# Conditioning vectors as VectorE dot products along rows of a transposed weight, in a two-block transformer kernel

## The chip, the cores and the metric

One core of a Trainium2 chip runs the whole program in one launch. The metric is the device time of one execution in microseconds. The kernel before takes 3524.61 us (median of three runs, 3524.37 to 3529.66). Engines are called as the profile calls them: PE (TensorE matmul), PEld (its weight load), DVE (VectorE), ACT (ScalarE), POOL (GpSimd), SP (SyncE, which issues the transfers).

## What is computed

`first_block` runs two layers on an image stream x (512 tokens by 1024) and a context stream of 256 tokens; `second_block` follows and is not touched. What the change is about is the conditioning: in each layer the vectors `c` and `c_ctx` pass through silu and are multiplied by `ada_w[l]` (1024 by 6144). The result, plus a bias, is cut into six vectors of 1024 that shift, scale and gate the two streams.

```python
for l in range(DEPTH):
    mod = (jax.nn.silu(c) @ ada_w[l] + ada_b[l])[:, None, :]
    sh1, sc1, g1, sh2, sc2, g2 = jnp.split(mod, 6, axis=-1)
    modc = jax.nn.silu(c_ctx) @ ada_w[l] + ada_b[l]
    shc1, scc1, gc1, shc2, scc2, gc2 = jnp.split(modc, 6, axis=-1)
    h = modulate(rms_norm(x, mix_pre_g[l]), sh1, sc1)
    hc = modulate(rms_norm(xc, mix_pre_g[l]), shc1, scc1)
    ...
    x = x + g1 * rms_norm(y, mix_post_g[l])
    h2 = modulate(rms_norm(x, ffn_pre_g[l]), sh2, sc2)
    x = x + g2 * rms_norm(sq_relu_mlp(h2, w_ff1[l], w_ff2[l]), ffn_post_g[l])
```

In the last layer only x is carried on, and of the context's six vectors only the first two are needed.

## The kernel before

Every large product is done in fp32 by three fp32r matmuls (`mm3`, L236 to L238): each operand is split into a high and a low part. A weight tile of 128x1024 (512 KB) is loaded by SP into a buffer `wr` (there are four, shared by everything that is called `wr`), ACT casts it into `wh` (L212), DVE subtracts to get `wl` (L215), and PE then runs 24 matmuls with it. `wh` and `wl` have four buffers each. SP issues in program order, so a load that waits for a buffer holds up the loads behind it.

Layer 0 runs in this order: the conditioning for the first norm (the first four column groups), keys and values, the mixer on x (about 120 to 725 us), the mixer on the context (about 800 to 1100 us), and the feed-forward on both (to about 1560 us). During the mixer on x the split weights are also written to DRAM (`wmode` "store"); the mixer on the context reads them back, 1 MB for each weight, straight into `wh` and `wl` or, for one in three, into two `wr` buffers (`wmode` "load"), and DVE has no `wl` to make there. The mixer's depthwise convolution of 31 taps is DVE work (L767), one instruction for each tap of each 128 channels.

The conditioning is in `ada_jobs`. A column group is 512 of the 6144 columns; a job `chunk` loads a 512 KB `wr` tile and multiplies it on PE against the silu vectors (L429, `ada`), four chunks to a group; then DVE copies the sums (L434), PE transposes them (L440, `adat`), and DVE folds and biases them into `mod` (L446, L447). Layer 0's groups 4 to 11 are spread through the mixer on x, among the convolution's jobs; layer 1's twelve groups are spread through layer 0's feed-forward. Background jobs are queued by `spread` and released by `tick` as the foreground weights go by; a scheduler then sets the final order on each engine.

In the feed-forward (`ff`), an up step runs one weight on both streams, and the result goes through ACT (relu, square), POOL (square in fp32, L932) and DVE (the low part, L935); a down step adds into `fy` on DVE (L950). The temporaries `relu`, `sq` and `csg` share a pair of buffers with tag `e`.

The lines of the code are quoted by program below.

## Time and profile before

| | |
|---|---|
| median of three runs | 3524.61 us (3524.37 to 3529.66) |
| the profiled execution | 3527.21 us, span 3525.4 us, granted PE clock 0.985 |
| PE busy | 3419.6 us, 97% |
| DVE busy | 2046.7 us, 58% |
| ACT, POOL busy | 1418.6 us (40%), 845.6 us (24%) |
| `ada` loads | 96 of 512 KB, 4.7 us to landing (median) |

Busy time is the time in which an engine has an instruction running. Matmuls overlap, and their ends are modelled, so what a matmul costs is read from the distance between two starts. The chain of waits follows the work that ended last backward from the end of the program.

### The profile page before, as it was taken

What the parts mean: (1) busy time and instruction counts of PE and PEld (TensorE: products, weight loads), DVE (VectorE), ACT (ScalarE), POOL (GpSimd) and SP (SyncE); (2) the same over time, 40 slices, a digit from 0 to 9 for tenths busy, and PEclk for the clock granted to TensorE, in tenths of its full rate; (3) what the DMA queues carried; (4) which work ended last, traced back from release to release, by engine and by line L of the source; (5) the groups of instructions that cost most, each with busy time, mean ns of one, the idle gap of its engine ahead of it and who ended that gap; (6) DMA issues with size and microseconds to landing.
All of it is one profiled execution on the core that took longest, in us unless ns stands there. A gap on an engine that the chain in (4) does not pass through costs nothing.

```text
span 3525.4 us, 54772 instructions
## 1 busy us (share of the span) xinstructions
PE 3419.6 (97%) x21313; PEld 2997.6 (85%) x21313; DVE 2046.7 (58%) x3652; ACT 1418.6 (40%) x2472; POOL 845.6 (24%) x931
## 2 busy tenths in 40 slices
PE   6999999989999999999899999999999899999999
PEld 4897887889999888899888898898888877789888
DVE  5567779656574323346757879756333757674334
ACT  4562332444223331234565243345323545544223
POOL 3230021232113110114421021234002336442002
PEclk8999999999999999999999999999999999999999
DMA  8527879786995533343411222244333420054333
GB/s 287 185 73 259 311 273 333 287 321 253 349 355 214 169 118 119 122 143 131 151 37 37 96 96 87 93 147 134 98 100 110 139 95 1 1 168 121 99 98 120
DMA packets 176419, 557.90 MB, mean 158 GB/s; under 512 B 18464, under 2 KB 43424, under 8 KB 176032
## 3 DMA queue, kind: packets, MB, share of 16 engines
q1 hardware_dynamic: 176160, 554.41, 45.6%
q8 instruction: 168, 2.75, 0.3%
q14 instruction: 91, 0.75, 0.1%
HBM read 436.89 MB, written 117.44 MB: 157 GB/s over the span
## 4 chain that ended last, share of the span: by engine, by line
PE 91%; ACT 3%; DVE 2%; DMA 2%; POOL 1%; issue 1%; SPq 0%; POOLq 0%; ACTq 0%; DVEq 0%
PE f L236 12%; PE f L238 12%; PE f L237 12%; PE pg L236 3%; PE pb L236 3%; PE pg L237 3%; PE pg L238 3%; PE pb L238 3%; PE pb L237 3%; PE c L236 2%; PE c L238 2%; PE c L237 2%; PE ada L429 1%; PE wo L236 1%; PE wo L237 1%; PE wo L238 1%
## 5 line engine op out<-in xcount | busy, mean ns | idle before, releaser
L212 ACT CAST wh<-wr 128x1024 fp32r<-128x1024 f32 (+1 forms) x486 | 508.8, 1049 | 1240.4 <-PE f L237 500.7
L215 DVE TENSOR_TENSOR wl<-wr,wh 128x1024 fp32r<-128x1024 f32 (+1 forms) x486 | 629.3, 1296 | 538.5 <-ACT wh L212 530.3
L767 DVE SCALAR_TENSOR_TENSOR yx<-gl,pcol,yx 128x512 f32<-128x512 f32 x480 | 368.0, 770 | 10.3
L932 POOL TENSOR_TENSOR relu<-relu 128x512 f32<-128x512 f32 (+1 forms) x146 | 137.9, 946 | 904.3 <-ACT hxh L931 592.7
L236 PE MATMUL f<-hxh,wh 128*128 128x512 f32 x576 | 226.0, 394 | 0.0
L238 PE MATMUL f<-hxh,wl 128*128 128x512 f32 x576 | 223.7, 389 | 0.0
L237 PE MATMUL f<-hxl,wh 128*128 128x512 f32 x576 | 223.6, 389 | 0.0
L236 PE MATMUL f<-hx2h,wh 128*128 128x512 f32 (+1 forms) x584 | 213.4, 369 | 1.1 <-ACT hx2h L317 1.0
L238 PE MATMUL f<-hx2h,wl 128*128 128x512 f32 (+1 forms) x584 | 212.2, 365 | 0.0
L237 PE MATMUL f<-hx2l,wh 128*128 128x512 f32 (+1 forms) x584 | 211.9, 364 | 0.0
L950 DVE TENSOR_TENSOR fyx<-f,fyx 128x256 f32<-128x256 f32 x144 | 56.1, 420 | 173.1 <-PE f L238 173.0
L278 POOL TENSOR_TENSOR sm<-sm,mhalf 128x2 f32<-128x2 f32 (+4 forms) x89 | 91.9, 1035 | 252.5 <-DVE sm L276 248.0
L236 PEld LDWEIGHTS f<-hxh,wh 128*128 128x128 f32 x576 | 108.1, 188 | 28.1 <-issue 5.4
L236 PEld LDWEIGHTS f<-hx2h,wh 128*128 128x128 f32 x584 | 110.2, 190 | 23.2 <-issue 2.1
L238 PEld LDWEIGHTS f<-hxh,wl 128*128 128x128 f32 x576 | 108.1, 188 | 22.9
L237 PEld LDWEIGHTS f<-hxl,wh 128*128 128x128 f32 x576 | 108.2, 188 | 21.8
L238 PEld LDWEIGHTS f<-hx2h,wl 128*128 128x128 f32 x584 | 110.8, 190 | 17.5
L237 PEld LDWEIGHTS f<-hx2l,wh 128*128 128x128 f32 x584 | 110.7, 190 | 16.5
L592 POOL TENSOR_SCALAR p<-p,sm 128x768 f32<-128x768 f32 (+1 forms) x80 | 65.7, 821 | 204.9 <-DVE sm L591 162.3
L935 DVE TENSOR_TENSOR hxl<-relu,hxh 128x512 fp32r<-128x512 f32 (+1 forms) x90 | 55.3, 616 | 101.5 <-POOL relu L932 101.5
L679 POOL TENSOR_TENSOR mx<-mx,sg 128x512 f32<-128x512 f32 x32 | 50.9, 1591 | 263.8 <-DVE sg L678 263.8
L236 PE MATMUL f<-h4h,wh 128*128 128x512 f32 (+1 forms) x328 | 112.5, 343 | 0.0
(718 smaller groups left out, 10622.8 us busy)
## 6 DMA issues: line engine op xcount, KB each, us to landing
wr<-in_w_ff_dram SPq DMA_DIRECT2D x234, 512.0 KB, 3.5
wr<-in_w_in_dram SPq DMA_DIRECT2D x141, 512.0 KB, 3.9
wr<-in_ada_w_dram SPq DMA_DIRECT2D x96, 512.0 KB, 4.7
wd<-wh SPq DMA_DIRECT2D x96, 512.0 KB, 3.9
wd<-wl SPq DMA_DIRECT2D x96, 512.0 KB, 4.2
wr<-wd SPq DMA_DIRECT2D x64, 512.0 KB, 4.6
wh<-wd SPq DMA_DIRECT2D x64, 512.0 KB, 4.1
wl<-wd SPq DMA_DIRECT2D x64, 512.0 KB, 5.1
```

The costliest lines, as they stand in the source:

```text
L212: nc.scalar.copy(hi, raw)
L215: eng.tensor_tensor(lo, raw, hi.bitcast(F32), ALU.subtract)
L236: mm(ps, a[0], b[0], start=start, stop=False)
L237: mm(ps, a[0], b[1], start=False, stop=False)
L238: mm(ps, a[1], b[0], start=False, stop=stop)
L278: nc.gpsimd.tensor_tensor(r, v, self.mhalf[0:rows].to_broadcast([rows, n]), ALU.pow)
L592: nc.gpsimd.tensor_scalar(p[:, :W], p[:, :W], rc, 1.0, op0=ALU.mult, op1=ALU.mult)
L679: nc.gpsimd.tensor_tensor(merged.k(k), merged.k(k), sg.k(k), ALU.add)
L767: nc.vector.scalar_tensor_tensor(Y.k(k), src, w, Y.k(k), op0=ALU.mult, op1=ALU.add)
L932: nc.gpsimd.tensor_tensor(r, r, r, ALU.mult)
L935: nc.vector.tensor_tensor(lo.k(k)[:, o], r[:, a - c0:b - c0], hi.k(k)[:, o].bitcast(F32), ALU.subtract)
L950: nc.vector.tensor_add(y.k(k), p, y.k(k))
```

## The change

Only layer 0's first four column groups stay on PE. All other vectors are made by `ada_dot_jobs`: the weight is laid out transposed (`ada_wt`), so that a 128x1024 tile has 128 output columns on its partitions and all 1024 inputs along each row. A silu vector is broadcast to all partitions in two tiles `crow` of 512, which take the place of the rope tables `cos` and `sin` until those are loaded again. One job loads the next tile and makes two `tensor_tensor_reduce` on DVE with the tile loaded a job earlier, each over 512 elements with a running sum; the product itself goes to a `junk` tile with tag `e`. In the program each of the two is an instruction of 128x512 and one of 128x1 that reads the sum out (both stand as ISA).

There are 24 such jobs for x in the mixer on x, 24 for the context in the mixer on the context, and 80 in layer 0's feed-forward, where they start after the second pass instead of the first and are spread over 41 ticks instead of 45.

```diff
-    def ada_jobs(self, l, c0, c1):
+    def ada_jobs(self, c0, c1):
...
+    def ada_dot_jobs(self, *sets):
+        nc = self.nc
+        row, raws = [], []
+
+        def cond(x):
+            row[:] = [self.lp.tile([P, S], F32, tag=f"rope{u}", name=self.nm("crow")) for u in range(2)]
+            for u in range(2):
+                nc.sync.dma_start(row[u], self.I["crow"][x, u].partition_broadcast(P))
+                nc.scalar.activation(row[u], row[u], AF.Silu)
+
+        def load(l, x, c):
+            raw = self.wp.tile([P, KT * P], F32, tag="wr", bufs=NB["wr"], name=self.nm("wr"))
+            nc.sync.dma_start(raw, self.I["ada_wt"][l, c])
+            raws.append(raw)
+
+        def dot(l, x, c):
+            raw = raws.pop(0)
+            part = self.small(1)
+            acc = self.pcol[l][:, PC_ADAB + c:PC_ADAB + c + 1]
+            for u in range(2):
+                junk = self.e("junk")
+                dst = part if u == 0 else self.mod[l][:, c // 4, x, c % 4:c % 4 + 1]
+                nc.vector.tensor_tensor_reduce(junk, raw[:, u * S:(u + 1) * S], row[u], 1.0, acc,
+                                               ALU.mult, ALU.add, dst)
+                acc = part
+
+        todo = [(l, x, c) for l, x, c0, c1 in sets for c in range(c0, c1)]
+
+        def step(i):
+            if i < len(todo):
+                load(*todo[i])
+            if i and (i == 1 or todo[i - 1][1] != todo[i - 2][1]):
+                cond(todo[i - 1][1])
+            if i:
+                dot(*todo[i - 1])
+        return [lambda i=i: step(i) for i in range(len(todo) + 1)] + [row.clear]
...
-            if n == 0:
-                self.spread(jobs, 45.0)
+            if n == (0 if extra else 1):
+                self.spread(jobs, 45.0 if extra else 41.0)
...
-        jobs = self.ada_jobs(0, 0, 4)
+        jobs = self.ada_jobs(0, 4)
...
-            mg = self.mixer(sx, l, h[0], kvs, self.ada_jobs(0, 4, 12) if not last else (), folds)
+            mg = self.mixer(sx, l, h[0], kvs, self.ada_dot_jobs((0, 0, 16, 40)) if not last else (),
+                            lambda: folds(0))
...
-                mg = self.mixer(sc, l, h[1], [kvc], beside=list(pre))
+                mg = self.mixer(sc, l, h[1], [kvc], self.ada_dot_jobs((0, 1, 16, 40)), lambda: folds(1),
+                                beside=list(pre))
...
-                        self.ada_jobs(1, 0, 12) if not last else ())
+                        self.ada_dot_jobs((0, 1, 40, 48), (1, 1, 0, 16), (0, 0, 40, 48), (1, 0, 0, 48))
+                        + [self.setup_rope] if not last else ())
```

The folds of the vectors with the norms' gains move with them: those for x and for the context are made apart, and `G2` at the feed-forward's end.

On DVE, in the second up phase of layer 0's feed-forward, the order before is this (`hxl` and `hcl` are the low parts of the two streams' hidden values, `wl` the low part of the next weights, `adarow` the old conditioning):

```order
L935 TENSOR_TENSOR hxl_2557_13443<-relu_13438,hxh_2556_13440 128x512
L434 COPY adarow_13557<-ada_13317 128x256
L935 TENSOR_TENSOR hcl_2561_13475<-relu_13470,hch_2560_13472 128x256
L215 TENSOR_TENSOR wl_13645<-wr_13642,wh_13644 128x1024
L215 TENSOR_TENSOR wl_13722<-wr_13719,wh_13721 128x1024
L935 TENSOR_TENSOR hxl_2570_13525<-relu_13520,hxh_2569_13522 128x512
```

And this is the same place after the change (`junk` is the product of a dot, `sm` the sum of its first half, `mod` the finished column):

```order
L975 TENSOR_TENSOR hxl_2701_13227<-relu_13222,hxh_2700_13224 128x512
L215 TENSOR_TENSOR wl_13276<-wr_13273,wh_13275 128x1024
L483 ISA junk_13262,sm_13261<-wr_13184,crow_12576,pcol_93 128x512
L483 ISA sm_13261 128x1
L975 TENSOR_TENSOR hcl_2686_13175<-relu_13254,hch_2685_13172 128x256
L483 ISA junk_13264,mod_95<-wr_13184,crow_12577,sm_13261 128x512
L483 ISA mod_95 128x1
L483 ISA junk_13269,sm_13268<-wr_13259,crow_12576,pcol_93 128x512
L483 ISA sm_13268 128x1
L483 ISA junk_13271,mod_95<-wr_13259,crow_12577,sm_13268 128x512
L483 ISA mod_95 128x1
L215 TENSOR_TENSOR wl_13360<-wr_13357,wh_13359 128x1024
```

Between two `wl` there now stand three halves of dots or more. Moreover the program gives `wr_13357` the buffer of `wr_13259`, whose dot stands directly ahead of `wl_13360`, and gives `wr_13273` the buffer of `wr_13177`, whose dot stands directly ahead of the `hxl` above; this pattern repeats every two weights through the up phases.

On SP, in the mixer on the context, the loads before are only the stored weights, two for each weight:

```order
L205 DMA wh_9361<-wd_3946 128x1024
L205 DMA wl_9363<-wd_3947 128x1024
L205 DMA wh_9426<-wd_4177 128x1024
L205 DMA wl_9428<-wd_4178 128x1024
L205 DMA wr_9430<-wd_4187 128x1024
L205 DMA wr_9432<-wd_4188 128x1024
```

After the change a conditioning tile is queued among them:

```order
L205 DMA wh_9301<-wd_3911 128x1024
L205 DMA wl_9303<-wd_3912 128x1024
L473 DMA wr_9241<-in_ada_wt_dram 128x1024
L205 DMA wh_9373<-wd_4134 128x1024
L205 DMA wl_9375<-wd_4135 128x1024
L205 DMA wr_9297<-wd_3901 128x1024
```

Some six to nine stored tiles stand between two conditioning tiles there.

## Rows read from the trace of the kernel before

**Rows 1.** The page's first part: busy time, share of the span and instructions.

```profile
PE 3419.6 (97%) x21313; PEld 2997.6 (85%) x21313; DVE 2046.7 (58%) x3652; ACT 1418.6 (40%) x2472; POOL 845.6 (24%) x931
```

**Rows 2.** The page's fourth part: the chain that ended last, by engine.

```profile
PE 91%; ACT 3%; DVE 2%; DMA 2%; POOL 1%; issue 1%; SPq 0%; POOLq 0%; ACTq 0%; DVEq 0%
```

**Rows 3.** Windows of three stages: stretch, length, busy us by engine, PEclk, DMA, GB/s.

```profile
290.00:650.00 360.00, 360.00 (x1945) 292.81 (x1944) 287.54 (x418) 110.13 (x158) 40.26 (x45) 1.00 0.85 309
...
850.00:1090.00 240.00, 238.59 (x1991) 238.39 (x1992) 148.71 (x355) 56.95 (x130) 28.14 (x44) 1.00 0.94 346
...
1170.00:1520.00 350.00, 350.00 (x2178) 292.53 (x2178) 97.14 (x206) 83.78 (x133) 29.95 (x35) 1.00 0.39 126
```

**Rows 4.** Windows of the tile `ada` alone: PE, PEld, DVE; eight records to a chunk.

```profile
290.00:650.00 360.00, 18.93 (x232) 5.22 (x232) 3.34 (x8) 1.00 0.85 309
...
1090.00:1170.00 80.00, 5.50 (x60) 1.46 (x60) 0.42 (x1) 1.00 0.46 155
1170.00:1520.00 350.00, 25.35 (x324) 7.29 (x324) 4.67 (x11) 1.00 0.39 126
```

**Rows 5.** Timeline of PE around one chunk in the feed-forward: start, us, what.

```profile
1395.07 0.28 PE L237 MATMUL f<-hcl,wh 128*128 128x256 f32 x1
1395.19 0.28 PE L238 MATMUL f<-hch,wl 128*128 128x256 f32 x1
1395.40 0.64 PE L429 MATMUL ada<-wr,adast 128*32 128x256 f32 x8
1395.97 0.50 PE L236 MATMUL f<-hx2h,wh 128*128 128x512 f32 x1
1396.31 0.39 PE L237 MATMUL f<-hx2l,wh 128*128 128x512 f32 x1
1396.54 0.40 PE L238 MATMUL f<-hx2h,wl 128*128 128x512 f32 x1
```

**Rows 6.** Windows of the tile `adat` alone, mixer on x: PE, PEld, DVE.

```profile
290.00:650.00 360.00, 3.04 (x16) 2.17 (x16) 2.98 (x32) 1.00 0.85 309
```

**Rows 7.** DVE instructions near to a dot: by line (ns min/median/max), and timeline.

```profile
L767 DVE SCALAR_TENSOR_TENSOR yx<-gl,pcol,yx x480: 737/752/1782, 275.6 to 2236.8; 128x512 f32<-128x512 f32 x160
...
L591 DVE RECIPROCAL sm<-sm x80: 152/164/167, 125.8 to 1900.2; 128x1 f32<-128x1 f32 x80
...
511.99 3.10 DVE L767 SCALAR_TENSOR_TENSOR yx<-gl,pcol,yx 128x512 f32<-128x512 f32 x4
...
0.79 0.06 DVE L371 MEMSET mhalf<- 128x1 f32 x1 [0.79 <-PEq L2053]
```

**Rows 8.** DVE in the mixer on x by line: busy us, mean ns, idle before.

```profile
L215 DVE TENSOR_TENSOR wl<-wr,wh 128x1024 fp32r<-128x1024 f32 x59 | 77.4, 1312 | 39.6 <-ACT wh L212 37.1 <-PE sv L714 1.2 <-DMA wd<-wl 1.0
```

**Rows 9.** Two windows of 10 us, columns as in rows 3.

```profile
530.00:540.00 10.00, 10.00 (x56) 7.51 (x56) 10.00 (x14) 5.02 (x6) 2.60 (x2) 1.00 0.75 264
...
990.00:1000.00 10.00, 10.00 (x86) 10.00 (x85) 9.41 (x21) 0.39 (x1) 1.75 (x2) 1.00 0.99 369
```

**Rows 10.** Transfers from 850 to 1090 us.

```profile
DMA packets 23062, 83.16 MB, mean 346 GB/s; under 512 B 2560, under 2 KB 2560, under 8 KB 23040
```

**Rows 11.** Timeline of SP, ACT and DVE in the feed-forward around one weight.

```profile
1414.34 0.33 SPq L209 DMA_DIRECT2D wr<-in_w_ff_dram  x1
...
1418.38 1.05 ACT L212 CAST wh<-wr 128x1024 fp32r<-128x1024 f32 x1 [3.80 <-DMA wr<-in_w_ff_dram]
...
1419.46 1.23 DVE L215 TENSOR_TENSOR wl<-wr,wh 128x1024 fp32r<-128x1024 f32 x1 [3.73 <-ACT wh L212]
1422.83 0.69 DVE L935 TENSOR_TENSOR hxl<-relu,hxh 128x512 fp32r<-128x512 f32 x1 [2.14 <-POOL relu L932]
...
1426.95 0.43 DVE L935 TENSOR_TENSOR hcl<-relu,hch 128x256 fp32r<-128x256 f32 x1
```

**Rows 12.** Transfers from 290 to 650 us: issues, KB, median us to landing.

```profile
wr<-in_w_in_dram SPq DMA_DIRECT2D x38, 512.0 KB, 5.9
```

## Prediction

> **What bounds it now.** I read the busy table first, then the chain of waits, then windows by stage, and last the instructions around one conditioning chunk. PE is busy for 97% of the span [rows 1] and holds 91% of the chain [rows 2]. In the three stages that the change touches PE is never idle: 360.00 of 360 us in the mixer on x, 238.59 of 240 in the mixer on the context, 350.00 of 350 in layer 0's feed-forward [rows 3]. So whatever leaves PE there shortens the program, unless another resource fills the gap. The same rows name the candidates: DVE is busy for 287.54 of 360 us in the mixer on x, the DMA engines for 0.94 in the mixer on the context, and in the feed-forward both have room (97.14 of 350 us, 0.39).

> **What PE loses.** A chunk stands between two products in rows 5. Starts of 256-column matmuls are 0.12 us apart, so the next product would have started at 1395.31; it started at 1395.97, and its second matmul came 0.34 us later instead of 0.23. A chunk thus costs 0.66 + 0.11 = 0.77 us. Of 96 chunks 16 stay, so 80 go: 29 in the mixer on x, 48 in the feed-forward (60 and 324 records at eight each) [rows 4] and three ahead of them. 80 x 0.77 = 61.6 us. The transposes of 20 groups go too: 3.04 us busy for eight pairs, 0.38 a pair [rows 6], half of it under the next matmul's start as with any matmul; 20 x 0.2 = 4.0 us. PE is relieved of 65.6 us: 24 in the mixer on x, 39.4 in the feed-forward, the rest around them. The DVE work that goes with them (copies, reductions, about 1.1 us a group by rows 4 and 6 and two small adds) was beside PE and is worth nothing by itself; I only subtract it from DVE's load.

> **What a dot costs.** No row shows a `tensor_tensor_reduce`. Its half reads two fp32 tiles of 128x512 as a convolution tap does: 752 ns median, four in 3.10 us [rows 7]; to that comes reading the sum, between a 128x1 memset (0.06) and a 128x1 reciprocal (0.164) [rows 7]. That bounds a half between 0.73 (a tap started on another's heels, and nothing more) and 0.94. I take 0.80, nearer to the taps, since they too are chained one to the next. Twice that if the two sources could not be streamed at once; this is a rival below. A dot is 1.6 us, 128 dots 205 us, all on DVE.

> **Mixer on x.** 23 of the 24 dots fall into the stretch of rows 3. DVE then holds 287.5 - 8.8 + 23 x 1.6 = 315.5 us, while PE needs 360 - 24 = 336. DVE at 94% can still keep up, and a stretch with DVE at 10.00 of 10 did not idle PE [rows 9]; but before, DVE waited 37.1 us for casts of late weights [rows 8], and only 20 us of idle time are left. What is late next is `wl`, which PE waits for. Bounds of what is given back: 0 (all those waits were PE's own pace) and 24 (DVE takes over wholly). I take 12.

> **Mixer on the context.** The 24 tiles are new here: 24 x 0.524 = 12.6 MB on top of 83.16 [rows 10]. The old bytes held the DMA engines for 0.94 x 240 = 225.6 us [rows 3], so the new sum needs 259.7 us at a share of 1.00, such as rows 9 show at 369 GB/s, and 276 at 0.94. PE needs 238.6. Given back beyond the old 240: 20 at full share, 36 at the old share, and 0 if tiles and stored weights can be fetched before the stretch begins. I take 20. DVE's 148.7 + 38 us fit.

> **Feed-forward.** Transfers and DVE have room in the mean: 80 dots are 128 us on 97. But loads wait for the four `wr` buffers, and two of three are now a dot's. In the up phases the order shows the pattern of two weights: the load of the second goes into the buffer of a dot that ends directly ahead of its `wl`, that of the first into one freed directly ahead of the `hxl`. From issue to the end of `wl` such a load takes 1420.69 - 1414.34 = 6.35 us [rows 11]; nothing else stands on DVE in that time. Two weights then need 6.35 + (0.8 + 0.43 + 2.4) + 6.35 + (0.69 + 0.43 + 3.2) = 20.65 us on this ring, the small terms being `hxl`, `hcl` [rows 11] and eight halves. PE needs 2 x (24 x 0.23 + 24 x 0.12) = 16.8 us [rows 5]. The ring loses 3.85 us on each of four pairs in a phase, 15.4 us; three `wl` stand ready when the phase starts, a lead of some 6 us. So 9.4 us a phase, and 19 us for the two phases that hold dots. In the down phases the same count gives about 6 us for a weight against 8.4, and nothing is lost. Bounds: 0 (loads land while DVE waits for PE anyway) and 48 (below).

> The rest is small: four pairs of `crow` loads with their silu and some ten more table loads on ACT, at 40% busy [rows 1]; rope tables come back well before layer 1 needs them; the moved folds are DVE instructions of 128x8, as before.

> **Sum.** 65.6 - 12 - 20 - 19 = 14.6 us. The profiled execution took 3527.2 us (its span is 3525.4), so 3512.6; it stands 2.6 above the median, so **3510**. What one can tell from no change here is about 0.2%, 7 us: faster is below 3517.6, slower above 3531.6.

> **Rivals.**
> - *Nothing is given back.* PE stays the only bound, each wait hides as it did: 3527.2 - 65.6 - 2.6 = 3459. For it: PE never idled where DVE or DMA ran full for 10 us [rows 9]. Against it: the DMA floor of 259.7 us in the mixer on the context.
> - *The ring in the feed-forward decides, slower.* If a load takes 5.9 us to land, as in the busier mixer on x [rows 12], instead of the 4.04 of rows 11, the ring takes 8.2 us a weight and 24.35 a pair: 7.55 x 8 - 12 = 48 given back instead of 19, and 3539. The total turns at a ring of 22.5 us, a landing of about 5.0. For it: three tiles are now in flight for each weight. Against it: with them the DMA engines are at about half their share, and rows 12 were taken at 0.85.
> - *The half dot takes twice the time of a stream*, 0.11 + 2 x 0.69 = 1.5 us. The mixer on x then needs 348 us of DVE, over PE's 336, and gives back 30 instead of 12; the ring grows by 5.6 us a pair and gives back 64 instead of 19: 3573. Against it: taps with two fp32 sources run at 752 ns [rows 7]. For it: a tap keeps no sum. [...]
> - *Both mixers at their upper ends* (24 and 36 given back): 65.6 - 24 - 36 - 19 = 13.4 us lost, 3538.

> That the vectors are not moved at all can be excluded: in the changed order 4 `adarow` copies are left of 24, and 256 halves stand on DVE.

> **How the numbers follow.** Forecast 0.46, with its own range 3490 to 3530; nothing given back 0.16; the ring 0.15; the slow half 0.10; both mixers 0.13. Faster: 0.16 and most of the forecast's case, 0.40, so 0.56. Same: 0.06 of the forecast and 0.09 from the weak ends of the ring and the mixers, 0.15. Slower: the rest, 0.29. The range 3472 to 3548 leaves out the slow half (0.10) and the lower part of "nothing given back" (0.10).

> **What would show it.** The `ada` records on PE fall from 768 to 128, and the instructions on the dot's line have a mean near 0.7 us with their read-outs near 0.1; a mean of 1.4 is the slow half. In the mixer on x, right is DVE busy for over 90% and PE idle for some us behind `wl`; wrong is PE without a gap in 336 us. In the mixer on the context, right is a stretch some 20 us longer at a DMA share near 1.00, with PE waiting for `wh` or `wl` loads; the same 240 us would mean that the tiles found room. In the up phases, right are gaps of some 2 us on PE behind `wl` while DVE waits for a cast and SP for a dot; no gaps there would mean the ring is faster than I count. A time below 3472 or above 3548 is outside all of this but the slow half.

## The result, and the profile after

The changed kernel takes 3557.49 us (median of 4 runs, 3554.17 to 3560.78) against 3524.69 before: ratio 1.0088, interval 1.0072 to 1.0104. It is **33 us slower**; the forecast was 3510, with 3472 to 3548 as its range. The profiled execution has a span of 3554.9 us against 3525.4, so 29.5 of the 33 us can be looked for in the trace.

First the page of the changed kernel: busy time [rows 1], the chain by engine [rows 2], and two lines of the transfers (KB each, us to landing).

```profile
PE 3383.0 (95%) x20633; PEld 2996.4 (84%) x20633; DVE 2207.6 (62%) x4022; ACT 1431.6 (40%) x2490; POOL 852.7 (24%) x931
...
PE 78%; DVE 8%; DMA 6%; ACT 3%; issue 2%; POOL 2%; SPq 0%; POOLq 0%; ACTq 0%; DVEq 0%
...
wr<-in_ada_wt_dram SPq DMA_DIRECT2D x128, 512.0 KB, 4.6
...
wr<-wd SPq DMA_DIRECT2D x64, 512.0 KB, 6.5
```

PE has less to do and a smaller share; the chain, 91% PE before, now runs through DVE, DMA and ACT for 17% of the span (7% before). Where? The windows of the three stages [rows 3] (columns as there):

```profile
290.00:650.00 360.00, 352.90 (x1753) 300.33 (x1752) 317.47 (x457) 120.72 (x172) 52.49 (x50) 0.99 0.85 304
850.00:1090.00 240.00, 204.37 (x1610) 202.30 (x1609) 165.92 (x409) 43.77 (x93) 19.42 (x33) 0.92 0.87 336
1170.00:1520.00 350.00, 325.08 (x1851) 283.66 (x1850) 185.49 (x402) 93.74 (x159) 46.72 (x52) 0.99 0.47 155
```

PE is idle for 7 us in the first, 36 in the second and 25 in the third, where it had no or 1.4 us of idle time before. In the second its granted clock is 0.92 on average.

To compare executions whose stages start at different times I cut the span at the first matmul of certain tiles, which the view by tile gives (ns min/median/max, then first and last start). These are the cuts in the changed kernel: first product of `osh` (the mixer on x past its attention), of `wo` (its output), of `woc` (the context mixer's output), first up pass, first down product of x in the split last quarter.

```profile
L236 PE MATMUL pb<-osh,wh x176: 279/389/389, 298.6 to 2052.8; 128*128 128x512 f32 x128, 128*128 128x256 f32 x48
...
L236 PE MATMUL wo<-mxh,wh x256: 277/283/366, 715.4 to 2417.2; 128*128 128x256 f32 x128
...
L236 PE MATMUL woc<-mch,wh x40: 283/283/283, 1116.0 to 1135.8; 128*128 128x256 f32 x40
...
L236 PE MATMUL f<-hx2h,wh x584: 274/389/797, 1139.0 to 2733.6; 128*128 128x512 f32 x147, 128*128 128x256 f32 x48
...
L236 PE MATMUL f<-hhx,wh x384: 277/283/363, 1667.8 to 3550.2; 128*128 128x256 f32 x192
```

In the kernel before the same starts are 295.4, 724.2, 1076.1, 1099.1 and 1631.0. (The last down products of layer 0 end at 1677 us there; about 1560 is where the passes on both streams together end.) So:

| stretch | before | after | change | forecast |
|---|---|---|---|---|
| start | 295.4 | 298.6 | +3.2 | |
| mixer on x (`osh` to `wo`) | 428.8 | 416.8 | **-12.0** | -24 + 12 = -12 |
| mixer on the context (`wo` to `woc`) | 351.9 | 400.6 | **+48.7** | +20 |
| feed-forward (first up pass to the split) | 531.9 | 528.8 | **-3.1** | -39.4 + 19 = -20.4 |
| the rest | 1917.4 | 1910.1 | -7.3 | -2.2 |
| span | 3525.4 | 3554.9 | +29.5 | -14.6 |

One stage came as forecast in size; the context mixer misses by 28.7 us and the feed-forward by 17.3. The dot itself is as priced (view by source line):

```profile
L483 DVE CUSTOM_DVE_ANT_0 junk<-wr,crow,pcol x128: 733/746/1174, 269.0 to 1579.0; 128x512 f32<-128x512 f32 x128
L483 DVE DVE_READ_ACCUMULATOR2_ANT sm<- x128: 71/81/85, 269.6 to 1579.7; 128x1 f32 x128
```

746 + 81 = 827 ns for a half, against 0.80 us taken.

**The context mixer.** What PE waited for from 850 to 1116 us (us in total, times, longest), and what SyncE's queue waited for from 715 on:

```profile
PE pg L236 <- DMA wr<-wd: 11.7, 2, 8.9
PE gv L236 <- DMA wr<-wd: 7.4, 1, 7.4
PE c L236 <- DMA wr<-wd: 6.3, 1, 6.3
PE pb L236 <- DMA wr<-wd: 4.0, 2, 3.4
PE gu L236 <- DMA wr<-wd: 3.3, 1, 3.3
```
```profile
SPq L205 <- PE pb L238: 40.6, 19, 6.7
...
SPq L473 <- DVE mod L483: 25.8, 5, 20.8
...
SPq L205 <- DVE mod L483: 18.0, 7, 4.8
```

Every one of PE's long waits is for a stored weight that was to land in a `wr` buffer, none for one in `wh` or `wl`; and the queue waits for dots to let `wr` buffers go. (Its larger waits, for PE to let `wh` and `wl` go, it had before too: 46.7 us for `pb`. Those for dots are new.) Transfers were not always the limit either: 10-us windows stand at a share of 1.03 and at 0.28.

```profile
880.00:890.00 10.00, 4.62 (x39) 4.41 (x37) 9.39 (x21) 0.77 (x2) 0.00 (x0) 0.86 1.03 413
...
940.00:950.00 10.00, 10.00 (x78) 10.00 (x78) 0.76 (x2) 1.79 (x6) 0.00 (x0) 0.91 0.28 92
```

**The feed-forward.** PE's waits from 1139 to 1668 us, and the timeline of the queue, of ACT and of DVE around the longest gap (start, us, in brackets idle before and releaser):

```profile
PE f L236 <- ACT wh L212: 20.8, 14, 5.2
PE f L238 <- DVE wl L215: 4.1, 14, 0.3
```
```profile
1326.74 1.12 SPq L468 DMA_DIRECT2D crow<-in_crow_dram  x2
1327.91 0.43 SPq L473 DMA_DIRECT2D wr<-in_ada_wt_dram  x1
1333.69 0.33 SPq L209 DMA_DIRECT2D wr<-in_w_ff_dram  x1
...
1331.34 1.16 ACT L469 ACTIVATE crow<-crow 128x512 f32<-128x512 f32 x2
...
1336.78 1.05 ACT L212 CAST wh<-wr 128x1024 fp32r<-128x1024 f32 x1 [1.92 <-DMA wr<-in_w_ff_dram]
...
1332.00 0.75 DVE L483 CUSTOM_DVE_ANT_0 junk<-wr,crow,pcol 128x512 f32<-128x512 f32 x1 [4.29 <-ACT crow L469]
...
1333.58 0.08 DVE L483 DVE_READ_ACCUMULATOR2_ANT mod<- 128x1 f32 x1
```

The weight's load is issued at 1333.69, right after the dot that ends at 1333.66: it needed that dot's buffer. Here the dot itself was late, since the conditioning row changed streams and its load and silu stood ahead of it. The cast follows at 1336.78, and PE has been idle since 1332.7.

### The profile page after: what moved, and what is told of

Same layout as the page of the kernel before. It is cut to its first block, busy times and chain, and to the rows that moved or that the text cites. A ratio compares the mean times of both kernels' runs of the same rounds, so it can differ in the third digit from the quotient of the medians.

```text
span 3554.9 us, 53920 instructions
## 1 busy us (share of the span) xinstructions
PE 3383.0 (95%) x20633; PEld 2996.4 (84%) x20633; DVE 2207.6 (62%) x4022; ACT 1431.6 (40%) x2490; POOL 852.7 (24%) x931
## 4 chain that ended last, share of the span: by engine, by line
PE 78%; DVE 8%; DMA 6%; ACT 3%; issue 2%; POOL 2%; SPq 0%; POOLq 0%; ACTq 0%; DVEq 0%
PE f L236 10%; PE f L238 10%; PE f L237 10%; PE pg L236 3%; PE pb L236 3%; PE pb L237 3%; PE pb L238 2%; PE pg L237 2%; PE pg L238 2%; PE c L236 2%; PE c L238 2%; PE c L237 2%; DMA wr<-in_w_ff_dram 2%; DVE yx L807 2%; DVE junk L483 2%
## 5 line engine op out<-in xcount | busy, mean ns | idle before, releaser
L966 ACT ACTIVATE relu<-f 128x512 f32<-128x512 f32 (+1 forms) x146 | 72.0, 493 | 123.1 <-PE f L238 114.2
```

Source lines behind the costliest of these rows:

```text
L966: nc.scalar.activation(r, ps, AF.Relu)
```

## The experiments

**Theory 1:** the dots' tiles take turns with the weights in the four `wr` buffers, and SyncE's in-order queue waits for a VectorE that is late; weights are issued too late in both stages. **Rival A:** the bytes of the 24 added tiles, in the context mixer. **Rival B:** VectorE's time. The table holds every run: medians of 2 (e5, e6) to 10 executions, stretches as cut above from one profiled execution each, ratio to the kernel before on the same chip. The diffs show changed lines alone, shortened.

| run | us | ratio [interval] | mixer x | context | feed-forward |
|---|---|---|---|---|---|
| before | 3524.7 | | 428.8 | 351.9 | 531.9 |
| changed | 3557.5 | 1.0088 [1.0072, 1.0104] | 416.8 | 400.6 | 528.8 |
| e1 no loads | 3472.6 | 0.9847 [0.9833, 0.9862] | 404.4 | 362.2 | 493.1 |
| e2 short dots | 3535.4 | 1.0025 [1.0015, 1.0034] | 408.6 | 396.8 | 520.1 |
| e3 neither | 3462.6 | 0.9821 [0.9806, 0.9836] | 404.4 | 352.0 | 493.0 |
| e4 dots in feed-forward only | 3526.0 | 0.9998 [0.9989, 1.0008] | 422.6 | 358.3 | 530.2 |
| e5 short dots, few bytes | 3490.7 | 0.9897 [0.9877, 0.9917] | 404.4 | 373.9 | 506.7 |
| e6 dots alone in `wr` | 3545.7 | 1.0053 [1.0033, 1.0073] | 418.2 | 382.2 | 531.3 |
| e7 GpSimd's queue | 3567.1 | 1.0110 [1.0093, 1.0127] | 417.1 | 402.6 | 541.4 |
| e8 own buffers | 3561.9 | 1.0096 [1.0081, 1.0111] | 411.4 | 386.4 | 492.8 |
| e9 and `pwin` moved | 3526.1 | 1.0000 [0.9991, 1.0010] | 410.9 | 384.2 | 492.7 |
| e10 feed-forward only, own | 3513.0 | 0.9961 [0.9947, 0.9975] | 423.5 | 358.6 | 492.8 |
| e11 the same, SyncE's queue | 3508.5 | 0.9952 [0.9937, 0.9967] | 422.6 | 358.4 | 492.8 |
| e12 before, small pools | 3560.3 | 1.0098 [1.0083, 1.0113] | 436.4 | 359.8 | 534.5 |
| **e13 as e11, five buffers** | **3481.7** | 0.9872 [0.9857, 0.9887] | 423.0 | 352.0 | 493.1 |
| e14 before, five buffers | 3521.8 | 0.9989 [0.9979, 0.9999] | 429.6 | 350.3 | 532.6 |
| e15 own buffers, short dots | 3512.5 | 0.9952 [0.9937, 0.9968] | 404.4 | 383.7 | 492.8 |

### Loads or VectorE: e1, e2, e3

```diff
 e1 and e3:
-            raw = self.wp.tile([P, KT * P], F32, tag="wr", bufs=NB["wr"], name=self.nm("wr"))
-            nc.sync.dma_start(raw, self.I["ada_wt"][l, c])
-            raws.append(raw)
+            raws.append(None)
 e1 (in e3 on columns 0:8):
-  tensor_tensor_reduce(junk, raw[:, u * S:(u + 1) * S], row[u], 1.0, acc,
+  tensor_tensor_reduce(junk, row[u], row[u], 1.0, acc,
 e2:
+  tensor_tensor_reduce(junk[:, 0:8], raw[:, u * S:u * S + 8], row[u][:, 0:8], 1.0, acc,
```

> The dots stay on VectorE at full length (256 halves of 128x512), but they multiply the conditioning row with itself: the 128 weight tiles of 512 KB are not loaded and no wr buffer is taken (the conditioning vectors are other numbers). Theory 1 (the dot tiles sit in the wr buffers that the weights need, and SyncE's in-order queue waits for a late VectorE): nearly all comes back, 3475 to 3495 us; the context mixer's loss falls from 49 us to under 10 and the feed-forward part gains over 30 of its 39.4. Rival A (the bytes: 12.6 MB more in the mixer on the context at 369 GB/s are 34 us): the context mixer recovers 34 and the feed-forward part, whose transfers have a share of 0.54, stays nearly as it is: 3515 to 3525. Rival B (VectorE's time for the dots delays the lo splits and the gate work): little changes, above 3540.

> All loads and their buffers stay; each half dot reads 8 of its 512 columns, so VectorE spends about 0.15 us on one instead of 0.83 (the vectors are other numbers). Theory 1: a buffer is let go as soon as its dot's turn comes, and VectorE is late less often; the feed-forward part gains over 30 of 39.4 and the context mixer's loss falls below 20: 3490 to 3510. Rival A (bytes): the context mixer's loss stays at 34 or more; with the feed-forward part as after, 3540 to 3550. Rival B (VectorE's time): everything comes back, 3460 to 3480.

> Neither loads nor full-length dots (8 columns of the row with itself): what is left is TensorE's relief of 65.6 us without what is given back. All theories: 3459 us, within 10. If it is well above, a part of the loss comes from something else than the dots and their loads: the order of the work, the conditioning row's loads, or the time in which the granted clock falls.

Without loads 85 us come back (3472.6), without VectorE's work only 22, without both 95. It is the loads, or the buffers that they take. With neither, the relief of PE stands bare: 428.8 - 404.4 = 24.4 us in the mixer on x and 531.9 - 493.0 = 38.9 in the feed-forward, as forecast (24 and 39.4). In the feed-forward the full dots without loads cost nothing (493.1), though VectorE is busy for 295.55 us there:

```profile
1089.00:1582.00 493.00, 493.00 (x2907) 438.80 (x2906) 295.55 (x596) 165.16 (x275) 97.12 (x98) 1.00 0.28 93
```

As a cause by itself rival B falls there and in the mixer on x (404.4 with full dots and no loads). In the context mixer VectorE's time alone costs 10 us (e1 against e3), and with loads in shared buffers short dots bring 8 or 9 us in the other two stages (e2). Rival A falls for the feed-forward, where it expected no change from e1. In the context mixer e2 keeps 45 of the 49 us, which A expected and theory 1 did not.

### The same stage with the mixers undone: e4

```diff
-  mg = self.mixer(sx, l, h[0], kvs, self.ada_dot_jobs((0, 0, 16, 40)) if not last else (),
+  mg = self.mixer(sx, l, h[0], kvs, self.ada_jobs(4, 10) if not last else (),
-  mg = self.mixer(sc, l, h[1], [kvc], self.ada_dot_jobs((0, 1, 16, 40)), lambda: folds(1),
+  mg = self.mixer(sc, l, h[1], [kvc], (), lambda: folds(1),
```

> The dots of both mixers (columns 16 to 40 of block 0, for both streams) go back to TensorE as six chunks in the mixer on x; the 80 dots in the feed-forward part stay as in the changed kernel. Both mixers then cost what they cost before, less two chunks of about 3 us of TensorE each; the feed-forward part saves 3 us as in the changed kernel; the later parts are 7 us quicker: 3525 - 6 - 3 - 7 = 3509 us (range 3500 to 3520). If the feed-forward part's loss hung on the late start that the context mixer gives it, it would save more: under 3490.

The feed-forward loses by itself (530.2), so its loss doesn't hang on a late start. The total missed by 17 us: the first 300 us took 5 us more, the context mixer 6 more, although it holds no dot, and the later parts gave 4 us instead of 7. Differences of under 10 us in the context mixer are therefore not read as prices below.

### Bytes, buffers, queue: e5 to e8

```diff
 e5 (e2, and):
-  nc.sync.dma_start(raw, self.I["ada_wt"][l, c])
+  nc.sync.dma_start(raw[:, 0:8], self.I["ada_wt"][l, c][:, 0:8])
 e6:
-  for u, tag in enumerate(("wr", "wr") if self.wcount % 3 == 0 else ("wh", "wl")):
+  for u, tag in enumerate(("wh", "wl")):
 e7 and e8:
-  nc.sync.dma_start(raw, self.I["ada_wt"][l, c])
+  nc.gpsimd.dma_start(raw, self.I["ada_wt"][l, c])
 e8:
-  raw = self.wp.tile([P, KT * P], F32, tag="wr", bufs=NB["wr"], name=self.nm("wr"))
+  raw = self.wp.tile([P, KT * P], F32, tag="dr", bufs=2, name=self.nm("dr"))
-  NB = {"n": 5, "e": 2, "wr": 4, "wh": 4, "wl": 4, "gl": 3, "sm": 32, "t": 51}
+  NB = {"n": 5, "e": 2, "wr": 3, "wh": 4, "wl": 4, "gl": 3, "sm": 32, "t": 49}
```

> As the run with short dots (3535 us; from the first matmul of the mixer on x's output to that of the context's: 397 us, before: 352), but each load of a weight tile brings 8 of its 1024 columns (32 bytes a partition); buffers, their order and the queue stay (the vectors are other numbers). Rival A (bytes): the 397 us of the context mixer fall by about 34 to some 363, the feed-forward part stays at 520 us: some 3500. Theory 1 (buffers and SyncE's order, whatever the bytes): 385 to 397 us there, 3525 to 3535 in all.

> The changed kernel, with the stored weights of the context mixer never put into the wr pair (always wh and wl): the dots have the four wr buffers to themselves there, so SyncE waits only for a dot four jobs back. The pairs loaded ahead fall from six to four. Theory 1: the context mixer's interval falls from 401 us to 365 to 380, the rest stays: 3522 to 3537. Rival A (bytes): it stays at 390 or above, or grows by the smaller depth: 3547 or more.

> The changed kernel, with the dots' weight tiles loaded from GpSimd's queue instead of SyncE's; same buffers in the same turn. Theory 1 has two halves. If SyncE's blocked queue is the cost, the context mixer's interval falls from 401 to some 375 and the feed-forward part (529 us, before 532, without loads 493) falls too: 3500 to 3520. If it is the turn of the four buffers, a weight's buffer still comes after the dots': the feed-forward part stays within 10 us of 529; in all 3530 to 3560. Rival A (bytes): no change in either, 3550 to 3560.

> The changed kernel, with two buffers of their own for the dots' tiles, loaded from GpSimd's queue; to make room the weights' wr buffers are three instead of four and the small tiles 49 instead of 51. Theory 1: the feed-forward part falls from 529 us to 495 to 505, and the context mixer to what the bytes alone leave (352 with none, at most 386 with 34 us of bytes): 3490 to 3515. Rival A (bytes): context mixer 386 to 400, feed-forward part unchanged: 3540 to 3560. Rival C (the smaller pools, or a GpSimd queue that waits for VectorE, cost as much as the ring did): above 3550.

e8 is the plainest answer: with own buffers the feed-forward takes 492.8 us, with full dots and all bytes. The total did not follow, because the attention of the second block grew by 38 us; its wide tiles `psel` and `pwin` also live in `wr`, where there were now three (e9 tests this). e7 speaks against the half of theory 1 on SyncE's queue: with the dots' loads in another queue but the same buffers, the context mixer stays (402.6), and the feed-forward gets worse; its total of 3567 lies above what either theory expected. e5 shows that the load's duration counts even where the transfers have room (a mean share of 0.49 in e2's feed-forward): a tile of 4 KB lands in 1.7 us there instead of 4.6 (e2), and the feed-forward falls from 520.1 to 506.7, since the buffer's turn is shorter. In the context mixer both theories are partly right: few bytes bring 23 us (e5 against e2), no shared buffers 18 (e6, whose 382.2 lies between the 380 and the 390 that the two expected).

### Own buffers without the side effect: e9 to e12

```diff
 e9 (e8, and), e10 (e4 and e8, and), e12 (the kernel before with this room):
-  pr[n] = [wide("wr", "psel"), wide("wr", "pwin"), self.t("pmid")]
+  pr[n] = [wide("wr", "psel"), wide("dr", "pwin"), self.t("pmid")]
 e11 (e10, and):
-  nc.gpsimd.dma_start(raw, self.I["ada_wt"][l, c])
+  nc.sync.dma_start(raw, self.I["ada_wt"][l, c])
```

> As the run with own buffers for the dots from GpSimd's queue (3562 us: feed-forward part 493 us, but the attention of the second block 38 us longer, since its wide tiles psel and pwin take turns in the wr buffers, three there instead of four); pwin now takes the two buffers that the dots had. Theory 1: that attention is as in the kernel before and the rest stays: 3562 - 38 = 3524 us (3515 to 3532). If the 49 small tiles were what cost it, nothing comes back: 3555 to 3565.

> Dots in the feed-forward part only (the mixers as in the kernel before, less two chunks), with two buffers of their own loaded from GpSimd's queue, pwin in those two later. Theory 1: feed-forward part starts at 1104 us and takes 493 instead of 530, what follows takes 1889 as in the run with neither: some 3489 us (3480 to 3498), faster than both kernels. Rival C (three wr buffers and 49 small tiles cost something in the mixers or the second block): 3500 to 3520.

> As the run before this one, but the dots' tiles are loaded from SyncE's queue, in front of the weights' loads: with two buffers each such load waits for the dot two jobs back, and the weights' loads wait behind it. If the buffers' turn was the whole cost in the feed-forward part: the same as from GpSimd's queue within 5 us. If SyncE's in-order queue behind a late VectorE costs by itself: the feed-forward part takes 510 us or more and the total is 15 us or more above.

> The kernel before with the same room (three wr buffers, 49 small tiles, pwin in two buffers of its own) and no dots: what the smaller pools cost or give by themselves. Theory 1: nothing beyond 10 us, 3520 to 3535. Rival C: 3540 or more.

e9 took 3526 for 3524. e10 and e11 have the same feed-forward, 492.8 us from either queue: sharing the four buffers is the whole loss there, and a SyncE queue that waits for VectorE costs nothing by itself. e10 missed its 3489, and e12 says why: three weight buffers instead of four cost the kernel before 34 us without a single dot, spread over start, both mixers and the step behind them. This is what rival C of the expectations said; theory 1 had allowed 10 us.

### Five buffers in turn, and bytes alone: e13 to e15

```diff
 e13 (e11, and) and e14 (e12, and):
+    def raw(self, name, dt=F32):
+        self.wturn += not self.dots
+        tag = "wr" if self.dots or self.wturn % 5 in (0, 2, 4) else "dr"
+        return self.wp.tile([P, KT * P], dt, tag=tag, bufs=NB[tag], name=self.nm(name))
 ...
+                self.dots = not last
                 self.ff(sts, h2, ...
 e15 (e9, and): the short dots of e2
```

All weights take their buffer from `raw`; `dots` is set in e13's feed-forward alone.

> Dots in the feed-forward part only, in two buffers of their own, from SyncE's queue (3509 us); outside that part the weights now take turns in all five buffers (three wr and the two of the dots) instead of three. If three buffers instead of four cost the chunks on TensorE their time in the mixers (first matmul of the mixer on x's output at 728 us instead of 723, start of the feed-forward part at 1118 instead of 1104) and in the first 300 us: it starts at 1104 or before, takes 493, then 1889: some 3489 us (3482 to 3500). If the 49 small tiles are what costs: no change, 3505 to 3515.

> The kernel before with the same five buffers in turn and no dots (with three it took 3560 us): what the room is worth by itself. If the weights' buffers set the time: 3515 to 3527, at or a little under the kernel before. If the 49 small tiles cost: above 3540. The difference to the run before this one is what the 80 dots are worth where they have room: 35 to 45 us.

> All dots, with two buffers of their own from GpSimd's queue and pwin there later (3526 us; context mixer 384 us), but each half dot reads 8 of 512 columns (the vectors are other numbers): all bytes, no shared buffers, hardly any VectorE time. If the context mixer's loss is made of bytes (23 us, from the short dots with and without bytes), VectorE's time (10 us, from the run without loads) and shared buffers (the rest): 352 + 23 = 375 us there, and the feed-forward part 493: 3512 to 3520 in all. If bytes alone are the 34 us at 369 GB/s: 384 to 386 there, no change in the total.

**e13 takes 3481.7 us, 1.3% less than the kernel before and 76 us less than the changed one.** The room alone is worth under 5 us (e14), the dots with room 40. The windows of e13's feed-forward, and what its SyncE queue waited for there (L480 loads a dot's tile, L490 is the dot):

```profile
1098.00:1591.00 493.00, 492.94 (x2905) 438.72 (x2904) 298.34 (x596) 164.99 (x276) 97.47 (x98) 1.00 0.52 179
```
```profile
SPq L480 <- DVE mod L490: 80.6, 58, 6.0
```

The queue still waits for dots, for 80.6 us, and PE does not notice.

e15 takes the shared buffers and VectorE's time out of the context mixer, and 383.7 us remain, the same as with full dots (384.2). Against the kernel before that is 32 us for the bytes. But e15 has three weight buffers, and with these the kernel before, which has no dots, takes 359.8 us (e12); against that it is 24 us, as e5 gave (23). The run e4 has four buffers and no dots in this stage and takes 358.3, so one execution can't say which base is right: the bytes cost 23 to 32 us. VectorE's time adds nothing where the bytes hold PE up already. The stretch in four kernels: before, before with three buffers (e12), own buffers (e9), and the changed one:

```profile
724.00:1076.00 352.00, 336.28 (x2726) 332.00 (x2725) 211.15 (x515) 118.65 (x271) 76.71 (x111) 0.97 0.87 322
```
```profile
736.70:1096.50 359.80, 339.34 (x2703) 333.65 (x2702) 212.25 (x513) 115.58 (x268) 75.67 (x110) 0.96 0.84 309
```
```profile
717.00:1102.00 385.00, 343.67 (x2708) 336.14 (x2707) 244.99 (x612) 119.28 (x272) 88.87 (x134) 0.95 0.87 326
```
```profile
715.00:1116.00 401.00, 349.54 (x2728) 343.36 (x2727) 246.23 (x614) 122.45 (x275) 76.06 (x111) 0.92 0.83 313
```

Length times rate gives 113.3 MB for before and 125.5 for e9 and the changed kernel. With own buffers the stretch runs at the share it had before, 0.87; with shared ones the share falls to 0.83. What the bytes don't explain, 16 to 25 us of the 48.7, goes with the shared buffers (e5, with tiles of 4 KB and VectorE busy for 219 us in the stage against 211 before, still loses 22), with some 4 us of VectorE's time in it (e2).

## Why the prediction was wrong, step by step

- **What PE loses** was right: e3 shows 24.4 and 38.9 us for 24 and 39.4; with nothing given back the kernel takes 3462.6 us, 3.6 above the rival's 3459.
- **What a dot costs** was right, 0.83 us a half for 0.80. The slow-half rival is out, and no run shows its 1.5 us: two fp32 sources in SBUF ran at 746 ns, as the taps do at 752 [rows 7], and the sum was read by an instruction of its own, 81 ns.
- **Mixer on x**: the size was right, 24.4 - 12.0 = 12.4 given back for 12 taken, and so was VectorE's load, 317.47 us for 315.5. The mechanism was not: PE was to wait for `wl`, and it never does. All its waits of more than 0.3 us from 299 to 715 us, and the stretch in the changed kernel and in e3:

```profile
PE cs L269 <- DVE cacc L827: 3.9, 1, 3.9
PE c L236 <- ACT wh L212: 3.2, 2, 2.8
```
```profile
298.60:715.40 416.80, 409.70 (x2009) 347.47 (x2008) 349.37 (x488) 149.45 (x211) 67.72 (x59) 0.99 0.84 302
297.90:702.30 404.40, 404.40 (x2009) 344.10 (x2008) 327.39 (x488) 147.05 (x209) 69.87 (x59) 1.00 0.78 283
```

PE waits 7.1 us, for one late reduction on VectorE and two casts, and is busy 5.3 us longer with as many matmuls. Full dots without loads give nothing back (e1), and neither do loads with short dots in own buffers (e15): it takes both. With own buffers and full dots 5.9 us come back (e9, 410.9) and 6.5 stay. That the sum of these was 12 is luck.
- **Mixer on the context** is the first step that failed: "I take 20". It priced bytes alone. They were there and cost 23 to 32 us, between the 20 and the upper bound of 36. The lower figure needed a share of 1.00 throughout, and a single window of 10 us that shows one [rows 9] is no ground for that: with the added bytes the stage ran at a mean share of 0.86 to 0.88 in the three measured kernels that kept dots and stored weights in separate buffers (0.88 in e6, 0.87 in e9, 0.86 in e15). The other 16 to 25 us are a mechanism that I had worked out for the feed-forward and did not look for here, though the stored weights use pairs of `wr` buffers too. Of the signs I named, the share was 0.83 and not near 1.00, and PE waited for stored weights in `wr`, not in `wh` or `wl`. The rival "both mixers at their upper ends" came nearest to this term, with 36 for 48.7.
- **Feed-forward**: the mechanism was right, the sum was not, 35.8 given back (528.8 - 493.0) for 19. The stretch in the changed kernel and in e3, then the changed kernel in pieces (columns of rows 3):

```profile
1139.00:1667.80 528.80, 503.88 (x2906) 442.80 (x2905) 296.24 (x596) 165.54 (x275) 94.44 (x98) 0.99 0.50 167
1077.30:1570.30 493.00, 493.00 (x2906) 438.82 (x2905) 215.92 (x596) 165.25 (x276) 96.41 (x98) 1.00 0.28 93
```
```profile
1290.00:1300.00 10.00, 8.53 (x35) 6.75 (x34) 5.38 (x11) 1.75 (x3) 1.23 (x2) 0.83 0.48 156
1300.00:1336.00 36.00, 29.13 (x167) 24.87 (x165) 16.91 (x35) 13.28 (x22) 7.60 (x8) 1.00 0.44 145
1336.00:1342.00 6.00, 4.12 (x12) 3.27 (x13) 4.76 (x11) 1.05 (x1) 0.00 (x0) 0.72 0.48 148
1342.00:1668.00 326.00, 311.31 (x1828) 274.59 (x1827) 191.87 (x396) 95.08 (x149) 53.41 (x53) 1.00 0.53 177
```

PE is idle for 24.9 us. One gap, 5.2 us, is the switch of streams, whose `crow` loads I had called small: they delay a dot, the dot holds a buffer, and PE stands. The other 19.7 us, from 1291 to 1370 and from 1445 to 1519 us, are the ring as counted (19). Besides, PE is busy 10.9 us longer with as many matmuls, a term that was missing. The clock is a part of it: windows at 0.83 of 10 us and 0.72 of 6 us hold 6.8 us at the lower level of 0.50, which cost 3.4 at most; in the last 326 us there are 14.7 us of gaps at a clock of 1.00. Another part is overlap lost at each stop: a matmul of 512 columns lasts 0.39 us, the next starts 0.23 after it [rows 5], so each of the 28 stops bares some 0.16 us, 4.5 in all (an estimate). What causes the last 3 us stays open.
- **The ring rival** ("decides, slower", 48 given back, from a landing of 5.9 us) had the right place; the weights landed in 4.1 us there at the median, for the 5.9 that it took.
- **The rest** was 7.3 us shorter for 2.2; I did not follow that up.

The range missed by 9 us: the context mixer went past its upper bound of 36 while the feed-forward gave back 17 us more than counted. Both share a cause, the four buffers, and no rival of mine moved the two together.

## What to carry to other kernels

When work moves to an idle engine, ask first through whose buffers its data comes: a loader that shares a ring with the critical weights can hold them up where engine and transfers are about half idle (in this feed-forward VectorE was busy for 296 of 529 us, at a DMA share of 0.50). In the feed-forward the same work with two buffers of its own gained 39 us instead of 3. One window at full share does not price added bytes: this stage held 0.86 to 0.88 with them. And room taken from another ring has its own price (34 us in e12), so time the old kernel with the new room before crediting the change, and compare each stage with the same room.

## What was not expected of the hardware

```profile
1330.00:1332.00 2.00, 2.00 (x19) 1.00 0.73 280
...
1338.00:1340.00 2.00, 2.00 (x5) 0.50 0.36 88
...
1342.00:1344.00 2.00, 2.00 (x10) 1.00 0.77 254
```

It did not do so after every gap: the ones behind 1342 us, of up to 1.9 us, left it at 1.00, while one of 1.2 us that ended at 1291.9 was followed by 0.50 from 1294 to 1296. In the context mixer the fall shows in windows of 4 us (same columns):

```profile
1034.00:1038.00 4.00, 2.12 (x18) 1.00 1.02 405
1038.00:1042.00 4.00, 0.00 (x0) 0.85 1.03 410
1042.00:1046.00 4.00, 0.95 (x4) 0.50 1.02 409
1046.00:1050.00 4.00, 4.00 (x21) 0.50 0.15 58
1050.00:1054.00 4.00, 4.00 (x31) 0.87 0.35 75
1054.00:1058.00 4.00, 4.00 (x36) 1.00 0.92 330
```

For the same 2726 to 2728 matmuls PE is busy 349.54 us in the changed kernel's context mixer and 336.28 before: 13 of the 48.7 us, on top of 36 more of idle time. In both stages PE lost more than the length of the gaps; in the feed-forward it was 10.9 us of busy time on 24.9 of idle time.

Left open: why GpSimd's queue with shared buffers makes the feed-forward 12.6 us longer (e7), and why the mixer on x loses its 12 us only where loads and full dots meet. Own buffers also meant five large buffers instead of four; no run lets dots and weights share five, so how much of the gain is the fifth buffer is not shown.
